# SSD decays from broadcast running sums instead of segment-sum matmuls

## The chip, the cores and the metric

The kernel runs on one core of a Trainium2 chip. The metric is device time in microseconds (us) of one execution. Its engines run side by side, each through its own fixed list of instructions: TensorE (PE, with PEld for its weight loads), VectorE (DVE), ScalarE (ACT), GpSimd (POOL) and SyncE (SP), which here only issues transfers. They wait for each other through semaphores, and each engine works strictly in the order of its list.

## The reference, cut to what matters

Two post-norm layers over 512 tokens and 1024 features: one Mamba-2 (SSD) mixer, one stick-breaking attention, each followed by a squared-ReLU MLP. The change touches the SSD mixer alone. Per head, with `a` the (negative) log decay of each time step, the mixer needs inside a chunk the matrix of decays between every two time steps:

```
def segsum(a):
    cs = jnp.cumsum(a, axis=-1)
    diff = cs[..., :, None] - cs[..., None, :]
    return jnp.where(mask, diff, -jnp.inf)        # mask: lower triangle
...
a = da...                                          # da = softplus(dt) * -exp(a_log)
a_cs = jnp.cumsum(a, axis=-1)
decay_mat = jnp.exp(segsum(a))
cb = jnp.einsum("bclgn,bcsgn->bcgls", cc, bc)
y_diag = jnp.einsum("bcgls,bcgrls,bcsgrp->bclgrp", cb, decay_mat, xc)
decay_states = jnp.exp(a_cs[..., -1:] - a_cs)
...
y_off = jnp.einsum("bclgn,bcgrpn,bcgrl->bclgrp", cc, prev, jnp.exp(a_cs))
```

There are 32 heads in 8 groups of 4; a group shares its B and C. All sums are over float32 values and the kernel keeps float32 accuracy.

## The kernel before, in words

**Numbers and matmuls.** Every float32 operand of a matmul is split in two: a high part rounded to the fast format (`fp32r`) and the rest, the low part. One product is then three matmuls (`mm3`, lines 208 to 210: high by high, low by high, high by low). Weights come in pieces of 128x1024 in the order of the list `stream`: SP fetches a piece into `wr` (tag raw, two buffers), ACT casts it to `wh` (line 191), and DVE, or POOL for one piece in four, subtracts to `wl` (line 193). `wh` and `wl` have four buffers each, so the cast of a piece waits until PE has finished with the piece four places earlier.

**Order of the work.** The program is traced as plain Python and a scheduler then fixes the list of each engine, taking pieces that are traced earlier first where it can; so the order on an engine is not the order of the text. Tile pools (`bufs=n`) set how many copies of a tile can be alive; PSUM has the tags `mm` and `bg` with four buffers each.

**The SSD mixer** (`ssm`) handles the sequence as four chunks of 128 tokens (`c` = 0 to 3) and the heads as eight groups (`g` = 0 to 7). Before the groups, `time_steps` projects the time steps (`pdt`, 24 matmuls), transposes them (`pdtt`), computes softplus on small 128x128 tiles (`dtt1`, a chain of some twenty short DVE and ACT instructions, lines 636 to 648), and makes `da` = dt * a in two parts, `da_h` and `da_l`. From these it forms on PE the running sums over a chunk, `pacs` (a matmul with the triangle `tri_le`), and the totals, `ptot` (with ones); ACT turns them into `E`, `bdec` and `dec_s`.

For each group there are five projections of 24 (or 48 half-width) matmuls: B and C (`in_bc`: `pB`, `pC`), z (`in_z`: `pz`) and two for x (`in_x`: `px`). A projection of B, C or x is followed by a convolution (one ACT instruction at line 678, then three on DVE at line 680, the tile `ca_...`) and a SiLU. `in_xt` transposes x (`pxt`) and makes the scaled copies `dx`, `xd`, `xe`.

`decays` makes the decay block of each chunk, 128 rows s by 4 heads by 128 columns t. For chunk c: POOL selects twice (line 779), from `da_h` and from `da_l`, each spread along t by a zero step, zero where t < s: the tiles `dm`. PE multiplies both with the triangle `tri_gt` (lines 782 and 783), which sums over s < k <= t into the PSUM tile `sg`; ACT takes the exponential into the SBUF tile `dec` (line 785). `scores` makes the products C.B of the group (`cb`, 12 short matmuls), copies them to `cbm` (line 795), and POOL zeroes the upper part (line 796). `front` multiplies `dec` by `cbm` (line 807; DVE for chunks 0 to 2, POOL for chunk 3), splits the product into `W_h` (ACT, line 809) and `W_l` (DVE, line 810), and advances the state (`st`, `pv`, `pr`). `back` uses `W` and `pr` on PE (`py`, `po`) and gathers `yg`; `gate` and `finish` follow.

The loop over g runs `scores`, `front` and `back` of group g while the object `fill` deals out projection steps of group g+1 between them: `fill.run(4)` gives four steps of three matmuls. After the chunks come `in_xt` of the next group, `gate`, `decays` of the next group, and `finish`. After groups 3 and 7 the output projection `tok_out` (`so`) runs half the sum each.

Of the kernel before, what the change touches and what calls it, by code (L numbers as in the profile page):

```python
# [23 lines left out]
G = 8  # L24
# [11 lines left out]
def trunk(ctx: ExitStack, tc: tile.TileContext, io):  # L36
# [6 lines left out]
    ps = ctx.enter_context(tc.tile_pool(name="ps", bufs=4, space=PSUM))  # L43

# [22 lines left out]
    for _ in range(14):  # L67
# [6 lines left out]
    tri_gt = cp.tile([P, P], F32R, name="tri_gt")  # L74
    nc.gpsimd.affine_select(tri_gt, one, pattern=[[-1, P]], compare_op=ALU.is_gt, fill=0.0,
                            base=0, channel_multiplier=1)
# [71 lines left out]
    depth = [2]  # L148

# [57 lines left out]
    def mm3(out, a, b, start, stop, skip=False):  # L207
        nc.tensor.matmul(out, a[0], b[0], start=start, stop=False, skip_group_check=skip)  # L208
        nc.tensor.matmul(out, a[0], b[1], start=False, stop=False, skip_group_check=skip)  # L209
        return nc.tensor.matmul(out, a[1], b[0], start=False, stop=stop, skip_group_check=skip)  # L210
# [362 lines left out]
    def ssm(sp, nxt_ln):  # L573
# [49 lines left out]
        dec_s = small("dec_s")  # L623

        def time_steps():
            w = wdt
            pd = psum("mm", [P, T], "pdt")
            proj(pd, w, x_)
# [25 lines left out]
            nc.vector.tensor_sub(da_l, da, f(da_h))  # L654
            pa = psum("bg", CH, "pacs")
            pt_ = psum("bg", CH, "ptot")
            for o, l in ((pa, tri_le), (pt_, ones_r)):
                nc.tensor.matmul(o, l, da_h, start=True, stop=False)
                nc.tensor.matmul(o, l, da_l, start=False, stop=True)
            nc.scalar.activation(E, pa, AF.Exp)  # L660
# [109 lines left out]
        def decays(q, cs=range(NT)):  # L770
            g = q.g
            hs = slice(4 * g, 4 * g + 4)
            if cs[0] == 0:
                q.dec = []
            for c in cs:
                nm = f"{g}_{c}"
                dm = pair(f"dm{nm}", S4, "dm", 1)
                for o, i in zip(dm, (da_h, da_l)):
                    nc.gpsimd.affine_select(o, f(i[:, c, hs]).unsqueeze(2).to_broadcast(S4), pattern=[[0, 4], [1, P]],
                                            compare_op=ALU.is_ge, fill=0.0, base=0, channel_multiplier=-1)  # L780
                pseg = psum("bg", S4, f"sg{nm}")
                nc.tensor.matmul(pseg, tri_gt, dm[0], start=True, stop=False)
                nc.tensor.matmul(pseg, tri_gt, dm[1], start=False, stop=True)
                dec = sp.tile(S4, F32, tag="dec", name=f"dec{nm}", bufs=4)
                table_order("exp", nc.scalar.activation(dec, pseg, AF.Exp))
                q.dec.append(dec)
# [516 lines left out]
```

## Time and profile before

| | us |
|---|---|
| median of 3 runs | 1417.35 (1416.71 to 1418.65) |
| the profiled execution, its own time | 1416.35 |
| its span, first to last instruction | 1414.2 |
| PE busy in the span | 1389.0 |
| DVE busy | 1076.8 |
| ACT busy | 783.8 |
| POOL busy | 221.8 |

The profile is of one execution. Busy time is the time in which an engine's instructions run; a wait is put down to what ended it. PE's matmuls overlap: one of 512 columns lasts 0.39 us but the next starts 0.23 us after it, and it is the second number that counts in a row of matmuls. The SSD mixer takes about the first 470 us of the span: preparation to about 49 us, groups 0 to 3 to about 217 us with some 45 us each, `tok_out`, groups 4 to 7, `tok_out`. The granted TensorE clock was 0.997 on average.

### The profile page before, as it was taken

How to read it: one execution, taken by the hardware profiler on the slowest of the kernel's cores; microseconds unless marked ns; L12 is line 12 of the kernel's file. 1: busy time of each engine (PE TensorE's matmuls, PEld its weight loads, DVE VectorE, ACT ScalarE, POOL GpSimd, SP SyncE). 2: the span in 40 equal slices, each digit the busy share in tenths (PEclk: the TensorE clock that was granted, in tenths of full speed). 3: DMA queues.
4: the chain of work that ended last, by engine and by line, in shares of the span. 5: the costliest groups of instructions: out<-in, count | busy, mean ns of one | idle time of the engine just before them, and what ended most of it. 6: DMA issues, size and time to landing. Idle time of an engine off the chain costs nothing.

```text
span 1414.2 us, 19327 instructions
## 1 busy us (share of the span) xinstructions
PE 1389.0 (98%) x7414; PEld 1197.0 (85%) x7414; DVE 1076.8 (76%) x1530; ACT 783.8 (55%) x1264; POOL 221.8 (16%) x249
## 2 busy tenths in 40 slices
PE   9999999999999999999999999999999999999996
PEld 6898897889997988888888799899889888888885
DVE  5798898368887596785859868787877966858588
ACT  5556575246653363635445568898853636454463
POOL 2344555034443100000000200000000000000001
PEclk9999999999999999999999999999999999999998
DMA  5223222222223345455453521121223455454533
GB/s 186 76 77 133 70 66 75 89 81 70 74 65 107 115 162 169 159 162 166 134 169 116 163 90 47 44 75 46 75 90 120 134 179 164 149 168 139 168 116 123
DMA packets 46699, 162.99 MB, mean 115 GB/s; under 512 B 5520, under 2 KB 5776, under 8 KB 46608
## 3 DMA queue, kind: packets, MB, share of 16 engines
q1 hardware_dynamic: 44016, 157.44, 34.9%
q10 hardware_dynamic: 2592, 4.33, 1.0%
q8 instruction: 58, 0.95, 0.3%
q14 instruction: 33, 0.27, 0.1%
HBM read 159.65 MB, written 2.10 MB: 114 GB/s over the span
## 4 chain that ended last, share of the span: by engine, by line
PE 87%; DVE 7%; ACT 2%; DMA 2%; issue 1%; POOL 1%; ACTq 0%; SPq 0%; DVEq 0%; POOLq 0%
PE f L209 8%; PE f L210 8%; PE f L208 8%; PE X L210 3%; PE X L208 3%; PE X L209 3%; PE pz L208 2%; PE pz L210 2%; PE pz L209 2%; PE px L208 2%; PE px L209 2%; PE px L210 2%; PE Y L210 2%; PE Y L209 2%; PE Y L208 2%; PE z L1141 1%
## 5 line engine op out<-in xcount | busy, mean ns | idle before, releaser
L191 ACT CAST wh<-wr 128x1024 fp32r<-128x1024 f32 x235 | 246.6, 1050 | 326.1 <-DMA wr<-w 159.1
L193 DVE TENSOR_TENSOR wl<-wr,wh 128x1024 fp32r<-128x1024 f32 x218 | 268.6, 1233 | 181.6 <-ACT wh L191 180.8
L210 PE MATMUL f<-ln_hh,wl 128*128 128x512 f32 (+1 forms) x544 | 201.2, 371 | 0.0
L209 PE MATMUL f<-ln_hl,wh 128*128 128x512 f32 (+1 forms) x544 | 201.2, 371 | 0.0
L208 PE MATMUL f<-ln_hh,wh 128*128 128x512 f32 (+1 forms) x544 | 200.3, 371 | 0.0
L210 PEld LDWEIGHTS f<-ln_hh,wl 128*128 128x128 f32 x544 | 102.4, 188 | 17.8 <-DVE wl L193 0.4
L209 PEld LDWEIGHTS f<-ln_hl,wh 128*128 128x128 f32 x544 | 102.4, 188 | 17.7 <-DVE ln_hl L400 0.2
L208 PEld LDWEIGHTS f<-ln_hh,wh 128*128 128x128 f32 x544 | 102.0, 188 | 17.4
L348 POOL TENSOR_TENSOR ln_rs<-ln_sums 128x1 f32<-128x1 f32 (+1 forms) x6 | 3.1, 513 | 632.6 <-ACT lnr L346 632.6
L208 PE MATMUL X<-wh,hP 128*128 128x512 f32 x192 | 74.7, 389 | 0.0
L209 PE MATMUL X<-wl,hP 128*128 128x512 f32 x192 | 74.7, 389 | 0.0
L210 PE MATMUL X<-wh,l 128*128 128x512 f32 x192 | 74.0, 389 | 0.0
L210 PE MATMUL pz<-wh,x_l 128*128 128x256 f32 x256 | 72.7, 284 | 0.0
L209 PE MATMUL pz<-wl,x_h 128*128 128x256 f32 x256 | 72.6, 284 | 0.0
L208 PE MATMUL pz<-wh,x_h 128*128 128x256 f32 x256 | 72.4, 283 | 0.0
L461 ACT CAST hP<-r 128x512 fp32r<-128x512 f32 x80 | 48.1, 620 | 32.0 <-DVE r L473 31.1
L193 POOL TENSOR_TENSOR wl<-wr,wh 128x1024 fp32r<-128x1024 f32 x17 | 42.6, 2504 | 92.3 <-ACT wh L191 92.0
L208 PE MATMUL px<-x_h,wh 128*128 128x512 f32 x128 | 50.8, 397 | 0.0
L209 PE MATMUL px<-x_l,wh 128*128 128x512 f32 x128 | 50.3, 393 | 0.0
L210 PE MATMUL px<-x_h,wl 128*128 128x512 f32 x128 | 50.2, 392 | 0.0
L209 PE MATMUL Y<-wl,hP 128*128 128x512 f32 x128 | 49.8, 389 | 0.0
L209 PEld LDWEIGHTS pz<-wl,x_h 128*128 128x128 f32 x256 | 48.8, 190 | 0.9
(1365 smaller groups left out, 3923.0 us busy)
## 6 DMA issues: line engine op xcount, KB each, us to landing
wr<-w SPq DMA_DIRECT2D x160, 512.0 KB, 3.6
wr<-w_bc SPq DMA_DIRECT2D x16, 512.0 KB, 3.5
wr<-w_x SPq DMA_DIRECT2D x16, 512.0 KB, 3.5
wr<-w_z SPq DMA_DIRECT2D x16, 512.0 KB, 3.5
wr<-w_so SPq DMA_DIRECT2D x16, 512.0 KB, 3.5
rawa<-w SPq DMA_DIRECT2D x16, 512.0 KB, 3.7
rawc<-w SPq DMA_DIRECT2D x16, 512.0 KB, 4.4
wr<-w_qk SPq DMA_DIRECT2D x16, 512.0 KB, 3.5
```

The costliest lines, as they stand in the source:

```text
L191: nc.scalar.copy(hi, raw)
L193: eng.tensor_sub(lo, raw, f(hi))
L208: nc.tensor.matmul(out, a[0], b[0], start=start, stop=False, skip_group_check=skip)
L209: nc.tensor.matmul(out, a[0], b[1], start=False, stop=False, skip_group_check=skip)
L210: return nc.tensor.matmul(out, a[1], b[0], start=False, stop=stop, skip_group_check=skip)
L348: nc.gpsimd.tensor_add(rs, self.sq[:, t0:t1, 0], self.sq[:, t0:t1, 1])
L461: nc.scalar.copy(h, src)
L1141: w_end[0] = nc.tensor.matmul(zj, ntri_ge, x, start=False, stop=i == 1, skip_group_check=True).ins
```

## The change

The exponent of the decay block is now a difference of running sums, cs[t] - cs[s], as in the reference, with no matmul for it.

- `time_steps` gets two more short matmuls that form the running sums with heads and chunks on the partitions (`pcsr`), ACT copies them (`csr`), and SP writes them, 128x128 numbers, to a scratch in device memory, `cs_rows`. ACT also stores the negative running sums, `ncs` = -`pacs`.
- `spread(q, c)` replaces the making of `dm` and `sg`: SP reads the 512 running sums of chunk c and the four heads from `cs_rows` into all 128 partitions of a `dec` tile, DVE adds `ncs` (its own row's sum, spread along t), and POOL selects once, putting -1e30 where t < s. `decays` is then only the four exponentials on ACT. The 64 matmuls `sg`, the `tri_gt` triangle, and the select of `cbm` are gone; `front`'s product is on DVE for all four chunks.
- `dec` has six buffers and not four. The spreads of group g+1 are traced behind `front(q, c)` of group g, chunk by chunk. Where `tok_out` follows (between groups 3 and 4), the exponentials of the next group are traced behind `finish` and not ahead of it.
- At the start the projections of B and C of group 0 are traced interleaved with that of the time steps. The later half of `time_steps` (the sums and what follows) is traced behind the last matmul of B's projection of group 1, which is drawn ahead (`ahead`, `tc.issue_after(behind[0])`: PE may not issue the sums before that matmul).

```diff
-        def time_steps():
-            w = wdt
-            pd = psum("mm", [P, T], "pdt")
-            proj(pd, w, x_)
+        ncs = small("ncs")
+        cs_rows = dp.tile([NT, H, P], F32, name="cs_rows")
+
+        def time_steps(pd):
...
             nc.vector.tensor_sub(da_l, da, f(da_h))
+            yield
             pa = psum("bg", CH, "pacs")
             pt_ = psum("bg", CH, "ptot")
             for o, l in ((pa, tri_le), (pt_, ones_r)):
                 nc.tensor.matmul(o, l, da_h, start=True, stop=False)
                 nc.tensor.matmul(o, l, da_l, start=False, stop=True)
+            pr = psum("mm", [P, P], "pcsr")
+            for i, x in enumerate((da_h, da_l)):
+                nc.tensor.matmul(pr, x.rearrange("p c h -> p (c h)"), tri_le, start=i == 0, stop=i == 1)
+            rows = sp.tile([P, P], F32, name="csr")
+            nc.scalar.copy(rows, pr)
+            nc.sync.dma_start(cs_rows.rearrange("c h t -> (c h) t"), rows)
+            nc.scalar.activation(ncs, pa, AF.Copy, scale=-1.0)
...
-        def decays(q, cs=range(NT)):
+        def spread(q, c):
             g = q.g
-            hs = slice(4 * g, 4 * g + 4)
-            if cs[0] == 0:
+            if c == 0:
                 q.dec = []
-            for c in cs:
-                nm = f"{g}_{c}"
-                dm = pair(f"dm{nm}", S4, "dm", 1)
-                for o, i in zip(dm, (da_h, da_l)):
-                    nc.gpsimd.affine_select(o, f(i[:, c, hs]).unsqueeze(2).to_broadcast(S4), pattern=[[0, 4], [1, P]],
-                                            compare_op=ALU.is_ge, fill=0.0, base=0, channel_multiplier=-1)
-                pseg = psum("bg", S4, f"sg{nm}")
-                nc.tensor.matmul(pseg, tri_gt, dm[0], start=True, stop=False)
-                nc.tensor.matmul(pseg, tri_gt, dm[1], start=False, stop=True)
-                dec = sp.tile(S4, F32, tag="dec", name=f"dec{nm}", bufs=4)
-                table_order("exp", nc.scalar.activation(dec, pseg, AF.Exp))
-                q.dec.append(dec)
+            dec = sp.tile(S4, F32, tag="dec", name=f"dec{g}_{c}", bufs=6)
+            nc.sync.dma_start(dec.rearrange("p h t -> p (h t)"),
+                              cs_rows[c, 4 * g:4 * g + 4, :].rearrange("h t -> (h t)").partition_broadcast(P))
+            nc.vector.tensor_tensor(dec, dec, ncs[:, c, 4 * g:4 * g + 4].unsqueeze(2).to_broadcast(S4), op=ALU.add)
+            nc.gpsimd.affine_select(dec, dec, pattern=[[0, 4], [1, P]], compare_op=ALU.is_ge, fill=-1e30,
+                                    base=0, channel_multiplier=-1)
+            q.dec.append(dec)
+
+        def decays(q):
+            for dec in q.dec:
+                table_order("exp", nc.scalar.activation(dec, dec, AF.Exp))
...
             nc.scalar.copy(q.cbm, pcb)
-            nc.gpsimd.affine_select(q.cbm, q.cbm, pattern=[[0, NT], [1, P]], compare_op=ALU.is_ge, fill=0.0,
-                                    base=0, channel_multiplier=-1)
...
-            eng = nc.gpsimd if c == 3 else nc.vector
-            eng.tensor_tensor(dec, dec, q.cbm[:, c, :].unsqueeze(1).to_broadcast(S4), op=ALU.mult)
+            nc.vector.tensor_tensor(dec, dec, q.cbm[:, c, :].unsqueeze(1).to_broadcast(S4), op=ALU.mult)
...
         cur = Group(0)
-        time_steps()
-        run(in_bc(cur, 0))
-        run(in_bc(cur, 1))
+        pd = psum("mm", [P, T], "pdt")
+        b_steps, c_steps = in_bc(cur, 0), in_bc(cur, 1)
+        for k, _ in enumerate(proj_steps(pd, wdt, x_)):
+            next(b_steps)
+            if k >= KD // 2:
+                next(c_steps)
+                next(c_steps)
+        steps = time_steps(pd)
+        next(steps)
+        run(b_steps)
+        run(c_steps)
         run(in_x(cur, 0))
         run(in_x(cur, 1))
+        ahead = Group(1)
+        b_steps = in_bc(ahead, 0)
+        for _ in range(KD):
+            next(b_steps)
+        with tc.issue_after(behind[0]):
+            run(steps)
+        for c in range(NT):
+            spread(cur, c)
         decays(cur)
...
+            def first(c):
+                front(q, c)
+                if nxt:
+                    spread(nxt, c)
...
-            if nxt:
+            if nxt and g % 4 < 3:
                 decays(nxt)
             finish(q, 1 if nxt else 2)
+            if nxt and g % 4 == 3:
+                decays(nxt)
```

Three places show what moves. In the lists a number behind a name is the tile's own; a digit in `pB1`, `pC1`, `px01` is the group (and half). The line numbers are those of each kernel's own text.

The first place is PE at the end of the preparation. Before, with most of C's projection of group 1 (`pC1`) ahead of the sums:

```order
L208 MATMUL pC1_553<-x_h_115,wh5_364 128x512
L209 MATMUL pC1_553<-x_l_116,wh5_364 128x512
L658 MATMUL pacs_224<-da_h_164,tri_le_98 128x128
L658 MATMUL ptot_225<-da_h_164,ones_r_76 128x128
L659 MATMUL pacs_224<-da_l_165,tri_le_98 128x128
L659 MATMUL ptot_225<-da_l_165,ones_r_76 128x128
L710 MATMUL pbt0_276<-ident_93,ca_B0_266 128x128 x3
L782 MATMUL sg0_0_403<-dm0_0h_399,tri_gt_100 128x512
L783 MATMUL sg0_0_403<-dm0_0l_400,tri_gt_100 128x512
L210 MATMUL pC1_553<-x_h_115,wl5_365 128x512
L208 MATMUL pz00_618<-wh6_485,x_h_115 128x256
```
After, beginning with the last matmuls of B's projection of group 1 (`pB1`):

```order
L207 MATMUL pB1_396<-x_h_115,wh4_318 128x512
L208 MATMUL pB1_396<-x_l_116,wh4_318 128x512
L209 MATMUL pB1_396<-x_h_115,wl4_319 128x512
L659 MATMUL pacs_421<-da_h_164,tri_le_100 128x128
L659 MATMUL ptot_422<-da_h_164,ones_r_78 128x128
L663 MATMUL pcsr_427<-tri_le_100,da_h_164 128x128
L743 MATMUL pxt00_471<-ident_95,ca_x00_347 128x128
L743 MATMUL pxt00_471<-ident_95,ca_x01_384 128x128
L743 MATMUL pxt00_471<-ident_95,ca_x00_347 128x128
```
The 24 matmuls of `pB1` stand ahead of the sums in both; the 23 of `pC1` that stood between them and the sums now stand behind, and the transposes `pxt` come between the sums of `da_h` and those of `da_l`.

The second place is DVE where it finishes the time steps. Before, from the end of the convolution of the second x tile of group 0 (`ca_x01`):

```order
L680 SCALAR_TENSOR_TENSOR ca_x01_393<-px01_368,cw_72,ca_x01_393 128x509
L646 SCALAR_TENSOR_TENSOR dtt1_201<-dtt1_201 128x128
L648 SCALAR_TENSOR_TENSOR dt_163<-dtt1_201 128x128
L652 SCALAR_TENSOR_TENSOR dtt2_202<-dt_163,dtt2_202 128x128
L653 CAST da_h_164<-dtt2_202 128x128
L654 TENSOR_TENSOR da_l_165<-dtt2_202,da_h_164 128x128
L193 TENSOR_TENSOR wl8_623<-wr8_620,wh8_622 128x1024
L664 TENSOR_TENSOR dtt2_202<-ptot_225,dtt2_202 128x128
L713 TENSOR_TENSOR bt0l_281<-pbt0_276,bt0h_280 128x384
L680 SCALAR_TENSOR_TENSOR ca_B1_529<-pB1_489,cw_72,ca_B1_529 128x511
L680 SCALAR_TENSOR_TENSOR ca_B1_529<-pB1_489,cw_72,ca_B1_529 128x510
L680 SCALAR_TENSOR_TENSOR ca_B1_529<-pB1_489,cw_72,ca_B1_529 128x509
```
After, from the split of a weight piece (`wl8`) on:

```order
L192 TENSOR_TENSOR wl8_599<-wr8_596,wh8_598 128x1024
L645 SCALAR_TENSOR_TENSOR dtt1_265<-dtt1_265 128x128
L688 SCALAR_TENSOR_TENSOR ca_B1_514<-pB1_396,cw_74,ca_B1_514 128x511
L645 SCALAR_TENSOR_TENSOR dtt1_265<-dtt1_265 128x128
L688 SCALAR_TENSOR_TENSOR ca_B1_514<-pB1_396,cw_74,ca_B1_514 128x510
L646 SCALAR_TENSOR_TENSOR dtt1_265<-dtt1_265 128x128
L688 SCALAR_TENSOR_TENSOR ca_B1_514<-pB1_396,cw_74,ca_B1_514 128x509
L648 SCALAR_TENSOR_TENSOR dt_163<-dtt1_265 128x128
L652 SCALAR_TENSOR_TENSOR dtt2_266<-dt_163,dtt2_266 128x128
L653 CAST da_h_164<-dtt2_266 128x128
L654 TENSOR_TENSOR da_l_165<-dtt2_266,da_h_164 128x128
```
The convolution `ca_B1`, which reads the finished projection `pB1` from PSUM, stood behind `da_h` and now stands ahead of it, woven into the chain of `dtt1`.

The third place is DVE around the first decay blocks. Before:

```order
L742 TENSOR_TENSOR xd0_435<-xt00_445,xd0_435 128x8x64
L680 SCALAR_TENSOR_TENSOR ca_C1_608<-pC1_553,cw_72,ca_C1_608 128x510
L742 TENSOR_TENSOR xd0_435<-xt01_458,xd0_435 128x8x64
L807 TENSOR_TENSOR dec0_0_406<-dec0_0_406,cbm0_480 128x512
L807 TENSOR_TENSOR dec0_1_415<-dec0_1_415,cbm0_480 128x512
L807 TENSOR_TENSOR dec0_2_424<-dec0_2_424,cbm0_480 128x512
L745 TENSOR_TENSOR xt00_445<-xt00_445,dec_s_168 128x512
L680 SCALAR_TENSOR_TENSOR ca_C1_608<-pC1_553,cw_72,ca_C1_608 128x509
L193 TENSOR_TENSOR wl11_849<-wr11_846,wh11_848 128x1024
L745 TENSOR_TENSOR xt01_458<-xt01_458,dec_s_168 128x256
L810 TENSOR_TENSOR W0_0l_504<-dec0_0_406,W0_0h_503 128x512
L810 TENSOR_TENSOR W0_1l_559<-dec0_1_415,W0_1h_558 128x512
```
After:

```order
L785 TENSOR_TENSOR dec0_1_445<-dec0_1_445,ncs_169 128x512
L785 TENSOR_TENSOR dec0_2_451<-dec0_2_451,ncs_169 128x512
L785 TENSOR_TENSOR dec0_3_457<-dec0_3_457,ncs_169 128x512
L688 SCALAR_TENSOR_TENSOR ca_C1_584<-pC1_538,cw_74,ca_C1_584 128x511
L756 TENSOR_TENSOR xe0l_469<-xt01_490,xe0h_468 128x256
L785 TENSOR_TENSOR dec1_0_566<-dec1_0_566,ncs_169 128x512
L810 TENSOR_TENSOR dec0_0_439<-dec0_0_439,cbm0_512 128x512
L688 SCALAR_TENSOR_TENSOR ca_C1_584<-pC1_538,cw_74,ca_C1_584 128x510
L785 TENSOR_TENSOR dec1_1_623<-dec1_1_623,ncs_169 128x512
L810 TENSOR_TENSOR dec0_1_445<-dec0_1_445,cbm0_512 128x512
L688 SCALAR_TENSOR_TENSOR ca_C1_584<-pC1_538,cw_74,ca_C1_584 128x509
L813 TENSOR_TENSOR W0_0l_553<-dec0_0_439,W0_0h_552 128x512
```
The five additions of `ncs` (each behind its transfer) stand ahead of the first product with `cbm0`; a sixth stands ahead of the first `W0_0l`.

More of the change, by code (lines that the diff above doesn't have):

```diff
@@ L43, in trunk @@
     ps = ctx.enter_context(tc.tile_pool(name="ps", bufs=4, space=PSUM))
+    dp = ctx.enter_context(tc.tile_pool(name="dp", bufs=1, space=bass.MemoryType.DRAM))
     def psum(tag, shape, name):
@@ L73, in trunk @@
                             base=0, channel_multiplier=-1)
-    tri_gt = cp.tile([P, P], F32R, name="tri_gt")
-    nc.gpsimd.affine_select(tri_gt, one, pattern=[[-1, P]], compare_op=ALU.is_gt, fill=0.0,
-                            base=0, channel_multiplier=1)
     none_r = cp.tile([P, P], F32R, name="none_r")
@@ L148, in trunk @@
     depth = [2]
+    behind = [None]
     def emit_w():
@@ L209, in mm3 @@
         nc.tensor.matmul(out, a[0], b[1], start=False, stop=False, skip_group_check=skip)
-        return nc.tensor.matmul(out, a[1], b[0], start=False, stop=stop, skip_group_check=skip)
+        end = nc.tensor.matmul(out, a[1], b[0], start=False, stop=stop, skip_group_check=skip)
+        behind[0] = end.ins
+        return end
     def proj(out, w, r, c0=0, c1=T):
@@ L895, in ssm @@
                 yT = act_pair(f"yT{g}")
-            nxt = Group(g + 1) if g + 1 < G else None
+            nxt = (Group(g + 1) if g else ahead) if g + 1 < G else None
             q = cur
             if nxt:
-                fill.add(in_bc(nxt, 0))
+                fill.add(in_bc(nxt, 0) if g else b_steps)
                 fill.add(in_bc(nxt, 1))
@@ L904, in ssm @@
                 fill.add(in_x(nxt, 1))
+            def first(c):
+                front(q, c)
+                if nxt:
+                    spread(nxt, c)
             scores(q)
             fill.run(4)
-            front(q, 0)
+            first(0)
             fill.run(5)
-            front(q, 1)
+            first(1)
             fill.run(5)
@@ L912, in ssm @@
             fill.run(4)
-            front(q, 2)
+            first(2)
             fill.run(4)
@@ L916, in ssm @@
             fill.run(4)
-            front(q, 3)
+            first(3)
             fill.run(4)
@@ L946, in ssm @@
                 else:
-                    nxt_ln.load_rows(lambda j, c0: sp.tile(S4, F32, tag="dec", name=f"lnr{j}{c0}", bufs=4)
+                    nxt_ln.load_rows(lambda j, c0: sp.tile(S4, F32, tag="dec", name=f"lnr{j}{c0}", bufs=6)
                                      .rearrange("p a c -> p (a c)"), T)
```

## The prediction

> **What bounds the kernel now.** I read the page first (shares of busy time, then the chain that ended last).
>
> ```profile
> PE 1389.0 (98%) x7414; PEld 1197.0 (85%) x7414; DVE 1076.8 (76%) x1530; ACT 783.8 (55%) x1264; POOL 221.8 (16%) x249
> ...
> PE 87%; DVE 7%; ACT 2%; DMA 2%; issue 1%; POOL 1%; ACTq 0%; SPq 0%; DVEq 0%; POOLq 0%
> ```
>
> PE is busy for 98% of the span and carries 87% of the chain: a matmul that goes is time gained, unless PE then waits. Next came PE's waits in the first 475 us, the SSD mixer (waited for, total, times, longest).
>
> ```profile
> PE pyt L872 <- DVE yg L867: 1.4, 1, 1.4
> ...
> PE st L208 <- ACT dec L785: 1.0, 1, 1.0
> ```
>
> Apart from the first 16 us and the output projections these are the only ones over 0.4 us. So every new wait of PE counts in full. The stretches from one group's score product to the next (length; then busy PE, PEld, DVE, ACT, POOL; groups 1, 2, 3, 5, 6) show which engine is next:
>
> ```profile
> 106.10:150.80 44.70, 42.76 (x267) 37.79 (x265) 40.81 (x63) 27.29 (x50) 22.65 (x24) 1.00 0.34 117
> 150.80:193.40 42.60, 42.60 (x269) 38.14 (x267) 37.23 (x63) 27.09 (x50) 22.11 (x22) 1.00 0.24 75
> 193.40:237.10 43.70, 43.70 (x256) 38.28 (x254) 35.58 (x53) 24.27 (x45) 24.12 (x23) 1.00 0.20 61
> 327.80:372.80 45.00, 45.00 (x290) 40.70 (x288) 37.86 (x61) 27.51 (x49) 22.15 (x23) 1.00 0.23 71
> 372.80:413.10 40.30, 40.30 (x289) 37.73 (x287) 34.14 (x57) 26.08 (x49) 19.68 (x22) 1.00 0.21 66
> sum 216.30, PE 214.36 PEld 192.64 DVE 185.62 ACT 132.24 POOL 110.70; mean PE 42.87 PEld 38.53 DVE 37.12 ACT 26.45 POOL 22.14
> ```
>
> DVE is busy for 185.6 of 216.3 us, 86%, in group 1 for 91%. ACT and POOL are at 61% and 51%. The change takes from PE and gives to DVE.
>
> **PE's gain.** What the removed matmuls cost is their step in the chain, not their length:
>
> ```profile
> 48.49 0.35 PE pbt L710 x3
> 48.84 0.23 PE sg L782
> 49.07 0.23 PE sg L783
> ...
> 49.54 0.12 PE pz L208
> ```
>
> and their number stands in the answer on the tile `sg`, eight rows of eight, of which the first and the last are:
>
> ```profile
> L782 PE MATMUL sg<-dm_0h,tri_gt x8: 393/476/481, 48.6 to 398.9; 128*128 128x512 f32 x8
> ...
> L783 PE MATMUL sg<-dm_3l,tri_gt x8: 389/477/485, 59.9 to 412.6; 128*128 128x512 f32 x8
> ```
>
> 64 x 0.23 = 14.7 us off PE, 1.84 per group, all on the path. The wait of `st` for `dec` (1.0) falls too: it was for a PSUM buffer that `sg` held. Added are two 128-column matmuls `pcsr`, 2 x 0.12 = 0.2 us. Net -15.5 before any new wait.
>
> **First new wait: the sums behind `pB1`.** The lists show that PE now issues `pacs` right behind `pB1`, while DVE has the convolution of that same `pB1` ahead of `da_h`, which `pacs` reads. So PE must stand still from the end of `pB1` until the convolution and the rest of the chain are through. Before, five microseconds of `pC1` lay there. The rows, of PE (first), ACT (three, of which the first is a cast of a weight piece that waited for PE) and DVE:
>
> ```profile
> 42.71 0.39 PE L208 MATMUL pC<-x_h,wh 128*128 128x512 f32 x1
> ```
> ```profile
> 48.17 1.05 ACT L191 CAST wh<-wr 128x1024 fp32r<-128x1024 f32 x1 [2.12 <-PE pC L209]
> 49.24 1.28 ACT L660 ACT_TABLE_LOAD   x1
> 50.53 0.28 ACT L660 ACTIVATE E<-pacs 128x128 f32<-128x128 f32 x1
> ```
> ```profile
> 40.59 1.22 DVE L193 TENSOR_TENSOR wl<-wr,wh 128x1024 fp32r<-128x1024 f32 x1
> 41.72 0.28 DVE L645 SCALAR_TENSOR_TENSOR dtt<-dtt 128x128 f32<-128x128 f32 x1
> 41.92 0.74 DVE L680 SCALAR_TENSOR_TENSOR ca_x<-px,cw,ca_x 128x511 f32<-128x511 f32 x1
> 42.59 0.28 DVE L645 SCALAR_TENSOR_TENSOR dtt<-dtt 128x128 f32<-128x128 f32 x1
> ...
> 44.62 0.29 DVE L648 SCALAR_TENSOR_TENSOR dt<-dtt 128x128 f32<-128x128 f32 x1
> 44.95 0.29 DVE L652 SCALAR_TENSOR_TENSOR dtt<-dt,dtt 128x128 f32<-128x128 f32 x1
> 45.27 0.23 DVE L653 CAST da_h<-dtt 128x128 fp32r<-128x128 f32 x1
> ```
>
> PE's first row is where `pB1` had ended, 42.71. Three transposes `pbt` (0.35) move ahead of that point, so it ends at 43.06 now. ACT, in its order, first casts the piece `wh8`, whose buffer `pB1` holds until its end: 43.1 to 44.1. The convolution's ACT part runs meanwhile behind it. DVE has `wl8` next: 1.13 from one start to the next (45.3), then 0.20 for a step of the small chain, three convolution steps of 0.67 with two small ones between (47.9), `dt` 0.33, `da` 0.32, `da_h` 0.23: 48.8. PE waits 48.8 - 43.1 = 5.7 us. No row of before shows this wait, but its length follows from the order; it could be down to 5.0 if ACT takes the convolution early and `wl8` hides, up to 7 if DVE is late on arrival, which the order makes possible: two more pieces of work (`bt0l` and a third weight piece) lie ahead of it now. I take 5.7.
>
> **Second new wait: the way through device memory.** From 48.8 PE has 3 short sums, 8 transposes, 8 matmuls of `pC1`, 3 sums again; with 0.12 and 0.23 that ends at 52.3. Then 16 of `pC1` (3.7), 12 of `cb` (1.4), 80 half-width ones of `pz` (9.6) and 9 short ones (1.1): PE comes to the first `py`, which needs `W0_0l`, at 68.1. The other way: ACT stores `ncs`, loads a table (1.28), forms `E`, `bdec`, a copy and `csr`, each 0.28 or less: about 2.2 us, to 54.5. Then a write and a read, one after the other. No transfer of before is of this kind; the nearest rows are (KB each, median us to landing; and a queue with packets, MB, share of 16 engines):
>
> ```profile
> lnr<-lnrow ACTq DMA_DIRECT2D x12, 256.0 KB, 3.4
> ...
> out<-v SPq DMA_DIRECT2D x8, 256.0 KB, 2.0
> ```
> ```profile
> q10 hardware_dynamic: 2592, 4.33, 1.0%
> ```
>
> `lnr` is the same shape as a spread, one row into 128 partitions; `out` is a write four times as large. So the write lands at 56.5 and the first spread at 59.9. Each further one takes the engines 1% of 1414 us for 4.33 MB, or 0.85 us for 0.26 MB, so six have landed by 64.2. DVE then has ahead of the end of `W0_0l`: six additions, two products and `W0_0l` itself, 9 instructions of 128x512 with two operands, three steps of a convolution (2.0) and two small pieces (0.7). The nearest row for the nine:
>
> ```profile
> L807 DVE TENSOR_TENSOR dec<-dec,cbm x24: 676/680/2878, 66.8 to 420.6; 128x512 f32<-128x512 f32 x24
> ```
>
> 0.68 at the median, less the 0.07 by which neighbours overlap above, is 0.61 each: 5.5. Together 8.2 and about 0.5 for landings that come later than DVE: 68.6. PE would wait 0.5 us. The maximum of that row, 2.88, shows that such an instruction can take 2.2 more. I take 1.5; the ends are 0 (the write is small) and 5 (each transfer a microsecond slower and one such delay). Behind `W0_0l` come some nine microseconds of DVE until `pr0_0l` (eight at 0.61, two weight pieces at 1.13, six short ones), which PE needs 8.7 us after it starts `py` (by its list: 25 matmuls at 0.23, 16 at 0.12 and a dozen short ones); I put 1.0 there, 0 to 3.
>
> **DVE in the groups.** Each group gets four additions of `ncs` and the fourth product from POOL: 5 x 0.61 = 3.05 us. Over the five stretches DVE then needs 185.6 + 15.3 = 200.9 of 216.3 - 9.2 = 207.1 us, 97%, and in group 1 43.9 of 42.9. POOL's load falls (per group eight selects, the select of `cbm` and a product go, four selects come), which should shorten DVE's long cases. I take 0.5 us per group of new waiting for six groups, 3.0; the ends are 0 and 4.9 per group (DVE keeps all the idle time that it has, so each group grows by 3.05 where it should have fallen by 1.84).
>
> [...]
>
> **What costs nothing.** SP gets 33 more transfers, in the queue of the weights, and waits there for `dec` buffers with weight pieces behind. Cover: SP already waits far longer for the buffers of those pieces,
>
> ```profile
> SPq L167 <- DVE wl L193: 199.2, 34, 12.1
> ```
>
> so 33 x 0.85 = 28 us of transfers in some 400 fit. Without it a late spread holds DVE, about 1 us each. The exponentials stay 32 on ACT. POOL's work is off the path.
>
> **The sum.** -14.7 - 1.0 + 0.2 + 5.7 + 1.5 + 1.0 + 3.0 = -4.3. Against the profiled execution's own 1416.35 that is 1412.0; that execution lies 1.0 below the median of the runs, and I do not add this. About 0.2% (2.8 us) is what a measurement of this kernel tells from no change.
>
> **The rivals.**
> - *DVE becomes the bound* (slower). If DVE in each group keeps the 3.9 us of waiting it has in group 1, the five groups need 47.8, 44.2, 42.5, 44.8 and 41.1 us where PE needs 42.9, 40.8, 41.9, 43.2 and 38.5 (busy time + 3.05 + 3.9, and length - 1.84): 13.2 us, with a sixth group like these 15.8 and not 3.0. That gives 1425. It decides from about 3 us of kept waiting. For it: 97%. Against it: POOL's relief, and that the idle time above was partly slack.
> - *The cover holds better*: only the first wait is real, the rest is absorbed: -15.5 + 5.7 = -9.8, 1406.6. For it: PE had almost no wait at 86%. Against it: DVE's added work.
> - *The way through memory is slow*: the second wait is at its end of 5: 1415.5. For it: two dependent transfers, neither seen here. Against it: the `pz` cover of ten microseconds.
>
> **How the numbers follow.** Forecast 0.43 (1408.5 to 1415.5; four fifths of it faster by over 0.2%, the rest within), better cover 0.18 (nearly all faster), slow memory 0.12 (within), DVE-bound 0.25 (0.04 within, 0.21 slower), something unseen 0.02. So faster 0.52, within 0.2% 0.25, slower 0.23. The range 1406 to 1422 takes in the better cover at its low end and half of the DVE-bound case. The likeliest case gives 1412.
>
> **What would show it.** In the trace after: no `sg`; PE idle 5 to 7 us ahead of `pacs`, put down to `da_h`; a wait of `py` for `W_0l` of 0 to 5 us; DVE busy above 90% in group 1, with its time waiting for transfers of `dec` under 1 us each; stretches between score products some 1.5 us shorter. The prediction is wrong if `pacs` does not wait (then 1406), or if PE waits for DVE's `wl`, `W` or `pr` by microseconds in each group (then 1420 and more).

## The result, and the profile after

The changed kernel is slower. Its median is 1433.87 us (1433.37 to 1434.70, four runs) against 1417.21 us of before, measured beside it (1416.71 to 1418.65, four runs): a ratio of 1.0117, with an interval of 1.0103 to 1.0131. The forecast was 1412.0 with a range of 1406 to 1422. Each experiment below has its ratio to runs of before taken beside it; the medians of those runs lie between 1416.6 and 1417.5 us, so differences of about 1 us between experiments say nothing. A single run, 1961.3 us at a granted clock of 0.65 (the kernel with both edits and the bias, below), stands far from all others and no reading rests on it. The profiled execution after has a span of 1432.2 us, 18.0 more than before; the first matmul of the first MLP starts at 487.2 us where it started at 469.2, so the whole difference of these two executions lies in the SSD mixer.

The page of after, its row of engines and its row of the granted clock:

```profile
PE 1387.5 (97%) x7352; PEld 1195.5 (83%) x7352; DVE 1085.3 (76%) x1570; ACT 782.6 (55%) x1266; POOL 181.4 (13%) x200
...
PEclk9989999999999999999999999999999999999998
```

PE is still busy for 97%, and its busy time fell by only 1.5 us though 64 matmuls of 0.23 us are gone. The clock row says why to look further: its third slice (71 to 107 us) is 8, and no slice before the last was under 9 apart from that. Next PE's waits in the first 480 us (waited for, total, times, longest):

```profile
PE pbt L718 <- ACT ca_B L690: 7.9, 2, 7.6
PE pacs L659 <- DVE da_h L653: 6.3, 1, 6.3
PE pyt L875 <- DVE yg L870: 6.2, 4, 2.3
```

The sums wait for `da_h` as forecast. A second wait of 7.6 us stands not at `py` but at `pbt`, the transposes of B of group 1. And `pyt`, which waited once for 1.4 before, now waits four times. The next answer of after gives the granted clock by stretch (length; busy PE, PEld, DVE, ACT, POOL; clock; DMA share and GB/s):

```profile
31.00:48.30 17.30, 13.09 (x61) 10.49 (x58) 15.55 (x32) 12.94 (x18) 2.40 (x1) 1.00 0.39 112
48.30:55.10 6.80, 4.70 (x17) 4.22 (x18) 4.84 (x11) 0.62 (x1) 0.00 (x0) 0.50 0.17 67
55.10:75.60 20.50, 15.73 (x115) 14.70 (x113) 11.35 (x16) 8.53 (x17) 6.40 (x6) 1.00 0.39 106
75.60:85.80 10.20, 7.41 (x34) 7.41 (x35) 10.19 (x17) 6.14 (x11) 3.31 (x3) 0.50 0.32 105
```

Within each of the two long waits (44.1 to 50.4 us and 70.8 to 78.4) the clock falls to 0.50, and it stays there for 7 and for 10 us in all, so that the matmuls behind the wait run slowly too. It is so again at 256.5 to 263.3 and at 454.5 to 457.9; before, the mixer had no such stretch. What this does to a matmul is seen in the list of PE (start, length, instruction):

```profile
43.48 0.39 PE L208 MATMUL pB<-x_l,wh 128*128 128x512 f32 x1
43.70 0.39 PE L209 MATMUL pB<-x_h,wl 128*128 128x512 f32 x1
...
53.25 0.63 PE L208 MATMUL pC<-x_l,wh 128*128 128x512 f32 x1
53.68 0.63 PE L209 MATMUL pC<-x_h,wl 128*128 128x512 f32 x1
```

From one start to the next it is 0.22 us ahead of the wait and 0.43 behind it. Busy time hides this: a slow matmul counts as busy.

So PE's time up to the first `f` was split in three, for each kernel of the study, from the starts of all its matmuls: each step from one start to the next is compared with the median step of matmuls of that width in the same trace. What the medians add up to is "matmul steps"; what a step takes more while the clock is 0.50, up to once the median, is "half clock"; all the rest is waiting. The medians in the table are of all runs, the other columns of the one profiled execution; for "sums behind six projections" that was the fastest run (1422.0 us), for "fourth product on POOL" the slowest (1418.9).

| kernel | median us | first `f` at | matmul steps | half clock | waits and rest |
|---|---|---|---|---|---|
| before | 1417.2 | 469.2 | 448.1 | 0 | 21.1 |
| after | 1433.9 | 487.2 | 433.7 | 9.4 | 44.1 |
| sums behind six projections | 1423.1 | 473.9 | 433.8 | 5.2 | 34.9 |
| the same, fourth product on POOL | 1416.0 | 470.4 | 433.8 | 3.0 | 33.6 |
| the same, additions on ACT too | 1409.9 | 463.7 | 433.6 | 3.0 | 27.1 |
| before, with DVE's added load alone | 1425.8 | 479.1 | 447.9 | 5.5 | 25.7 |

The removed matmuls are worth 14.4 us in the steps, as forecast; 9.4 us at half clock and 23.0 us of waiting stand against them. PE's list names most of that waiting: the two waits of the start, and `pyt`. The three kernels in the middle and the last are experiments, below.

### The profile page after: what moved, and what is told of

It is laid out like the page before. It is cut to its first block, busy times and chain, and to the rows that moved or that the text cites. A ratio compares the mean times of both kernels' runs of the same rounds, so it can differ in the third digit from the quotient of the medians.

```text
span 1432.2 us, 19279 instructions
## 1 busy us (share of the span) xinstructions
PE 1387.5 (97%) x7352; PEld 1195.5 (83%) x7352; DVE 1085.3 (76%) x1570; ACT 782.6 (55%) x1266; POOL 181.4 (13%) x200
## 5 line engine op out<-in xcount | busy, mean ns | idle before, releaser
L209 PE MATMUL px<-x_h,wl 128*128 128x512 f32 x128 | 50.4, 394 | 0.0
L207 PEld LDWEIGHTS pz<-wh,x_h 128*128 128x128 f32 x256 | 49.6, 194 | 0.3
```

Source lines behind the costliest of these rows:

```text
L209: end = nc.tensor.matmul(out, a[1], b[0], start=False, stop=stop, skip_group_check=skip)
```

## The experiments

Theories. **A**: the loss is made at the start, by the two waits and the half clock behind each. **B**: DVE's added work in the groups turns PE's gain into waiting. **C**: the way through device memory sets the start. **D** (against a part of A): a wait costs its length and the clock behind it nothing more.

### The start: position of the sums, and the way through memory

Three kernels, with after the four corners of a square. First the sums are held behind the projection of C of group 1 as well, which stood ahead of them before:

```diff
-        b_steps = in_bc(ahead, 0)
-        for _ in range(KD):
-            next(b_steps)
+        b_steps, c_steps = in_bc(ahead, 0), in_bc(ahead, 1)
+        for s in (b_steps, c_steps):
+            for _ in range(KD):
+                next(s)
...
-                fill.add(in_bc(nxt, 1))
+                fill.add(in_bc(nxt, 1) if g else c_steps)
```

> The changed kernel with one thing moved: the sums stand behind six projections (C of group 1 too), so that the 6.3 us wait of PE for da_h is covered. Theory A (the waits at the start, and the half clock that follows each, make most of the loss): the wait ahead of pacs falls under 1 us and the half clock of 48 to 55 us goes; the way through device memory still ends at the same time, so PE waits for it some 5 to 8 us. About 8 us faster than the changed kernel, 1426, and still slower than before. Theory B (VectorE's added work in the groups is the bound): the start is absorbed later, 1432 to 1435. Theory C (the round trip through memory alone sets the start, what PE does ahead of it does not matter): the second wait grows by what the first loses, 1433.

Measured: 1423.11 us (1421.97 to 1424.18), ratio to before 1.0046 (1.0029 to 1.0063); 10.8 us off after. Its waits of PE:

```profile
PE pyt L875 <- DVE yg L870: 7.2, 3, 5.0
...
PE pacs L659 <- DVE da_h L653: 0.9, 1, 0.9
PE pbt L718 <- ACT ca_B L690: 0.6, 1, 0.6
```

Both waits at the start are down to under 1 us, and no stretch at half clock is left ahead of 235 us. Theory A asked for 8 us and a second wait of 5 to 8 that did not come; theory C is refuted in this place, for the transfers are all still there.

Second, after's start with the old way for group 0 alone (in `decays`: for `q.g == 0` the selects into `dm`, `sg` and the exponential of before; `cbm` selected for that group):

```diff
...
-        for c in range(NT):
-            spread(cur, c)
         decays(cur)
```

> The changed kernel, with the decays of group 0 alone by the old way (8 sg matmuls, selects of dm and cbm); groups 1 to 7 take the spread rows. The first wait stays. Theory A: the wait of pbt (7.6 us) and the half clock of 76 to 86 us (3.5 us lost beside waiting) go, sg costs 1.8: 9 us faster than the changed kernel, about 1425. Theory B: 1434 to 1437 (sg comes on top). Theory C: about 1428, since the round trip was 7.6 of the loss and the clock nothing.

Measured: 1427.64 us (1425.97 to 1428.35), ratio 1.0074 (1.0059 to 1.0089), 6.2 off after: theory C's number, 3 short of A's. The wait of `pbt` is gone, that of `pacs` (6.4) stands, with a stretch of 10.2 us at clock 0.50 that begins in it. Third, both edits:

> Both edits: the sums behind six projections and group 0 by the old way. Theory A: no wait over 1 us and no half clock in the first 100 us; 1417.2 - 12.9 (56 sg) + 0.2 + 5 (pyt waits) + 1 to 3 (later half clock) = about 1412, 1406 to 1417. Theory B: the groups still wait for VectorE, 1425 or more. Theory C: about 1418 (after less 14 of waits less 2, the rest being lost elsewhere).

Measured: 1423.73 us (1423.46 to 1424.17), ratio 1.0048 (1.0033 to 1.0063). That is 0.6 more than with the sums moved alone. So the way through memory costs some 6 us where the sums stand behind five projections, and nothing that shows behind six. (The edit is not the way through memory alone: it puts eight `sg` matmuls back, 1.8 us, and takes four additions off DVE in group 0.) And theory A is short: with no long wait at the start the kernel is still 7 us slower than before, where 5 faster was asked for. Something behind the start takes about 12 us.

### The clock by itself

The control pins C's matmuls of group 1 behind the sums and puts one matmul on constants ahead of them; the next kernel has 36 of those.

```diff
+            pr4 = psum("mm", [P, T], "pcsr")
+            pr = pr4[:, :P]
+            for _ in range(36):          # 1 in the control
+                nc.tensor.matmul(pr4[:, P:].rearrange("p (a c) -> p a c", a=3), ones_r,
+                                 ones_r.unsqueeze(1).to_broadcast([P, 3, P]), start=True, stop=True)
             pa = psum("bg", CH, "pacs")
...
-            fill.run(4)
+            if g == 0:
+                with tc.issue_after(sums_end[1]):
+                    fill.run(4)
+            else:
+                fill.run(4)
```

> Control for the next kernel: the changed kernel, with the matmuls of C of group 1 held behind the sums, and one matmul of 384 columns on constants put into the bank of pcsr ahead of the sums. The wait of PE for da_h stays at 6 to 6.5 us, the clock is halved from about 48 us on. 1430 to 1440 under every theory; it is what the next kernel is compared with.

> As the control, with 36 of these matmuls (0.17 us each, 6.1 us) in the place of one: PE does useless work in the time in which it would wait for da_h, and nothing else changes. Theory A (a wait also costs half the clock afterwards): no half clock at 48 to 55 us; the matmuls behind the sums run at 0.23, the sums reach ScalarE some 2 to 3 us earlier, and the kernel is 2 to 5 us faster than the control. Theory D (a wait costs its own length, no more): within 1 us of the control, or slower by up to 0.5 us where the useless matmuls run past da_h.

(`sums_end[1]` is the last matmul of the sums.) Measured: 1431.52 us (1428.57 to 1434.07) and 1432.05 us (1431.09 to 1433.27): no difference that shows. The same stretch in both, the control first:

```profile
47.20:54.00 6.80, 3.64 (x16) 3.54 (x17) 5.16 (x12) 0.86 (x2) 0.00 (x0) 0.50 0.28 77
```
```profile
47.20:54.00 6.80, 6.73 (x41) 5.86 (x40) 4.70 (x12) 3.06 (x8) 0.00 (x0) 1.00 0.22 78
```

The half clock there went, as theory A says, and the first `py` came at 68.7 and not 71.5 us (0.9 of that difference was there already at the first `px`). But both kernels reach the second group's `cb` at the same time, 110.5 and 110.7: over the mixer some 3.6 us less of half clock stand against waits that did not shrink by the 6 us that the useless matmuls fill, but by 2 (37.6 to 35.6). So the half clock is real, but here it was not what set the end of group 0; the time saved came back as waiting (in the second kernel that `cb` waits 2.4 us for DVE's `xt`, in the control not at all). Theory D's number came out, though not for its reason. Beyond the dummies the two lists differ a little in group 0.

### VectorE's load

Before, with DVE's added load alone:

```diff
+                nc.vector.tensor_tensor(dec, dec, one[:, 0:4].unsqueeze(2).to_broadcast(S4), op=ALU.mult)
                 q.dec.append(dec)
...
-            eng = nc.gpsimd if c == 3 else nc.vector
+            eng = nc.vector
```

> The kernel before, with VectorE's added load alone: each block of decays is multiplied by one on VectorE (512 columns, two operands, as the addition of ncs), and the fourth product goes from GpSimd to VectorE: five instructions of 0.61 us more per group, 24 us in all; sg and everything else stay. Theory B: PE waits for VectorE, 10 us or more slower than before, 1427 and up. Theory A: PE's time with sg leaves VectorE room; the prediction's term was 0.5 us per group, so 2 to 6 us slower than before.

Measured: 1425.83 us (1424.29 to 1427.25), ratio 1.0052 (1.0035 to 1.0069): 8.3 us slower than the runs beside it, between the two theories. In group 1 DVE is now the engine that hardly rests (columns as above):

```profile
109.28:154.97 45.69, 42.95 (x262) 37.59 (x260) 44.36 (x68) 25.90 (x49) 20.34 (x23) 1.00 0.32 114
```

DVE 44.36 of 45.69 us. This is the nearest test of the forecast's term of 3.0, with PE's own work unchanged; the multiplication by one also lengthens the chain from the exponential to the product, and the scheduler's order is another. In the table the loss stands as 5.5 us of half clock and 4.6 of waiting; the longest wait in the mixer that PE's list names is one of 2.1 for `pyt`. Next, in the kernel with both edits, the additions go to ACT as the bias of four exponentials of 128 columns:

```diff
-            nc.vector.tensor_tensor(dec, dec, ncs[:, c, 4 * g:4 * g + 4].unsqueeze(2).to_broadcast(S4), op=ALU.add)
...
-            for dec in q.dec:
-                table_order("exp", nc.scalar.activation(dec, dec, AF.Exp))
+            for c, dec in enumerate(q.dec):
+                for h in range(4):
+                    table_order("exp", nc.scalar.activation(dec[:, h, :], dec[:, h, :], AF.Exp,
+                                                            bias=ncs[:, c, 4 * q.g + h:4 * q.g + h + 1]))
```

> As the kernel with both edits, and the 28 additions of ncs are taken from VectorE: each exponential is issued as four of 128 columns with ncs as their bias, on ScalarE. VectorE loses 28 x 0.61 = 17 us, ScalarE gains about 28 x 0.6 = 17 us. Theory A: within 3 us of the kernel with both edits. Theory B: 5 to 15 us faster than it.

Measured: 1418.44 us, ratio 1.0011 (1.0001 to 1.0021): 5.3 faster than without, at the low end of theory B. Then the load of DVE was taken back whole (the additions to ACT as above, the fourth product to POOL), first with after's start:

```diff
-            nc.vector.tensor_tensor(dec, dec, q.cbm[:, c, :].unsqueeze(1).to_broadcast(S4), op=ALU.mult)
+            eng = nc.gpsimd if c == 3 else nc.vector
+            eng.tensor_tensor(dec, dec, q.cbm[:, c, :].unsqueeze(1).to_broadcast(S4), op=ALU.mult)
```

> The changed kernel with VectorE's load taken back to that of before: the additions of ncs go to ScalarE as the bias of four exponentials of 128 columns, the fourth product goes back to GpSimd. The start stays (sums behind five projections, both transfers). Theory A: the start's loss of some 11 us stays whole, the groups gain what the load cost before, 8 us: 1424 to 1427. Theory B (VectorE's load turns each gain of PE into waiting): the whole loss but the first wait goes, 1417 to 1422, since group 0 has room again to catch up.

Measured: 1427.58 us (1424.82 to 1429.44), ratio 1.0071 (1.0056 to 1.0086). Just above theory A's range, 6.3 off after; the waits at the start stand:

```profile
PE pacs L659 <- DVE da_h L653: 6.3, 1, 6.3
PE pbt L718 <- ACT ca_B L690: 5.2, 2, 3.8
```

The same with the sums behind six projections, and once more with group 0 by the old way:

> The same with the sums behind six projections: nothing is left of VectorE's added load, nor of the first wait. If the start (11 us) and the load (8 us) are the two causes and add up, 1433.9 - 11 - 8 = about 1415; if the removed matmuls then come through whole, 1417 - 14.5 + 3 = 1406. Above 1418 a third cause is missing (the end of group 3, where so was pulled forward).

> The same, and group 0 by the old way (8 sg, no spreads before the first products). Theory C (the round trip costs even behind six projections): 3 to 6 us faster than the kernel without this. Theories A and B: 0 to 2 us slower, by the 1.8 us of sg.

Measured: 1409.87 us (1409.00 to 1410.97), ratio 0.9947 (0.9930 to 0.9963): faster than before and than after, and between the two numbers named ahead of it (1415 and 1406). Its largest waits in the mixer are all under 2 us, and DVE, at 36.18 of 42.50 us in group 1, has room again:

```profile
PE st L208 <- DVE xe4l L756: 1.9, 1, 1.9
PE pbt L718 <- ACT ca_B L690: 1.9, 2, 1.3
PE py L850 <- DVE pv L825: 1.7, 1, 1.7
```
```profile
111.30:153.80 42.50, 41.50 (x264) 37.09 (x263) 36.18 (x58) 28.77 (x60) 17.75 (x18) 1.00 0.43 140
```

The old way for group 0 gives 1415.0 us, ratio 0.9986 (0.9976 to 0.9995), 5 slower: theory C fell a second time, but A and B (0 to 2 slower) missed as well. Its trace has a wait of `pyt` of 5.4 us at the end of group 3, with 10.2 us at clock 0.50 from 233.3 on; the light kernel has neither.

Which half of the relief counts? With the additions moved but the product left on DVE, and with the product moved but the additions left:

> The sums behind six projections, the additions on ScalarE, the fourth product still on VectorE (8 x 0.61 = 5 us of its load): between the kernel with the sums moved alone (1423.1) and the light one. Theory B: 1 to 3 us slower than the light one. Theory A: no difference.

> The sums behind six projections and the fourth product back on GpSimd, the additions of ncs on VectorE. In its order so is still pulled forward in group 3, as in the kernel with the sums moved alone (1423.1). If the product is the load that counts: 1410 to 1413, as the light kernel. If the order at the end of group 3 decides: 1418 to 1423, with a wait of pyt of 4 to 6 us there and half clock after it. If VectorE's whole load decides: between the two, about 1417.

Measured: 1423.18 us (1419.45 to 1427.76), ratio 1.0043 (1.0031 to 1.0054), for the first: a miss for both theories, it gains nothing over the sums moved alone and is 13 slower than the light kernel. And 1415.98 us (1414.05 to 1418.92), ratio 0.9990 (0.9981 to 1.0000), for the second: 7.1 off the sums moved alone, nearest to the number for DVE's whole load (1417). In it, the products on DVE (first row) and the one on POOL, which takes about twice as long (min, median, max in ns):

```profile
L811 DVE TENSOR_TENSOR dec<-dec,cbm x24: 675/680/1749, 68.8 to 422.3; 128x512 f32<-128x512 f32 x24
...
L811 POOL TENSOR_TENSOR dec<-dec,cbm x8: 1288/1298/2835, 71.6 to 419.9; 128x512 f32<-128x512 f32 x8
```

So behind six projections the product gains 7 us alone and 13 together with the additions; the additions gain 6 with the product moved and nothing without. The two are not independent, and they do not go with DVE's busy time. Up to the first `f` DVE is busy for 374.4 us with the sums moved alone, 372.5 with the product moved (7.1 faster), 355.6 with the additions moved (no faster) and 346.4 in the light kernel. The kernel with the additions moved loses in another place: its waits of `pyt` come to 9.5 us (1.4 in the light kernel) and its half clock to 7.9 (3.0), which is 13.0 of the 13.6 us by which its first `f` comes later. So DVE's load, as a number of busy microseconds, is not shown to be the cause; the order in which its results come at the end of a group is part of it.

### The end of group 3

In the kernels with the sums moved, the light one apart, PE draws matmuls of `so` (the output projection) forward into group 3, and `pyt` is left without cover at its end. In the kernel with both edits and the bias this is one wait, the only one of PE listed from 160 to 260 us:

```profile
PE pyt L897 <- DVE yg L892: 6.9, 1, 6.9
```

The first half of `so` was held behind the last `py` of that group, here and with the sums moved alone, and in the light kernel:

```diff
+                last_py[0] = nc.tensor.matmul(py[:, h, 0, :], ...).ins
...
+                    with tc.issue_after(last_py[0]):
+                        out(half)
```

> The kernel with both edits and the bias, and the first half of the output projection held behind the last py of group 3, so that its matmuls cover the end of that group (gate, root, pyt). Theory A: the wait of pyt (6.9 us) in group 3 and the half clock from 235 to 245 us (2.9 us beside waiting) go; what of so stood earlier in the group leaves waits of up to 4 us there. 4 to 9 us faster than the kernel with the bias, 1409 to 1414, and so faster than before. Theory B (VectorE is the bound in every group): the wait only moves to py and po of group 3; within 2 us of it, 1416 to 1420.

Measured: 1421.55 us (1420.36 to 1423.61), ratio 1.0028 (1.0019 to 1.0038), 3 slower than without (2.4 by the two ratios). The wait of `pyt` is gone, and waits inside the group stand in its place, with a stretch of 13.7 us at clock 0.50 among them:

```profile
PE py L872 <- DVE bt4l L724: 2.3, 1, 2.3
PE py L873 <- DVE W_0l L835: 1.0, 1, 1.0
PE py L872 <- DVE yg L866: 0.8, 1, 0.8
```

The two balance in the mixer: its first `f` comes at 468.4 us, without the edit at 468.9. What this execution loses lies behind the mixer, from the first `f` to the end, 950.0 us against 947.5 (945.0 in before and after); why is open.

> The sums behind six projections, so of the first half held behind the last py of group 3, no relief of VectorE. If the end of group 3 decides: the wait of pyt (5.0) and the half clock after it (3.6) go, 1413 to 1417. If VectorE's load decides: the wait moves into the group, to py and po, 1420 to 1424.

Measured: 1417.90 us (1415.11 to 1420.82), ratio 1.0007 (0.9997 to 1.0017): 5.2 faster than with the sums moved alone, without relief of DVE, and between the two numbers named ahead of it (the first `f` comes at 467.5 us, 6.4 earlier). A wait of `po` for `yg` of 3.2 us has come up inside the group.

> The light kernel with so held back too, where its order already has most of so late. Either theory: within 2 us of the light kernel's 1409.9.

Measured: 1410.98 us (1406.86 to 1413.51), ratio 0.9950 (0.9932 to 0.9968): no difference from the light kernel.

So the order at a group's end counts as well: holding `so` back gained 5 us in one kernel and nothing in two others. It cannot be taken apart from the load by these runs, since the scheduler writes another order for each load: in the kernel with only the product moved `so` stands drawn forward too, and no long wait followed. What is shown is the sum of the three edits, from after to the light kernel: 10.8 (start), 7.1 (product) and 6.1 (additions), 24.0 us in all. How much of the last two is DVE's time and how much the order that came with it stays open.

## Why the prediction was wrong, step by step

- **PE's gain, -14.7**: right; the steps of the matmuls fell by 14.4. The wait of `st` for `dec` went too.
- **First new wait, 5.7**: right in place, cause and size (6.3). DVE did what its list said: `da_h` at 50.12 behind the convolution of `pB1`.
- **Second new wait, 1.5 with ends 0 and 5**: wrong in place and size, 7.6 us, by several of its parts. The transfers were taken too short: the write took 3.4 and not 2.0 us, and the six spreads, issued 0.4 to 0.5 us apart, landed between 3.5 and 7.1 us after their issue, up to 1.9 us apart and not 0.85. One of DVE's additions, at 69 us, took 2.7 us where the median is 0.69: the single delay that the upper end had allowed for. And the list of PE was read only for `py`; `pbt` stands ahead of it, and its SiLU stands on ACT behind the first exponentials:

```profile
68.65 0.63 ACT L792 ACTIVATE dec<-dec 128x512 f32<-128x512 f32 x1 [1.15 <-POOL dec L786]
74.72 0.62 ACT L812 CAST W_0h<-dec 128x512 fp32r<-128x512 f32 x1 [5.44 <-DVE dec L810]
75.25 1.15 ACT L792 ACTIVATE dec<-dec 128x512 f32<-128x512 f32 x2
76.41 1.28 ACT L690 ACT_TABLE_LOAD   x1
77.71 0.63 ACT L690 ACTIVATE ca_B<-ca_B 128x512 f32<-128x512 f32 x1
```

  ACT waits for DVE's products, DVE for the spreads, and `ca_B`, which needs none of them, waits behind. The first wait made this worse: partly at half clock, the eight transposes and eight matmuls that stand between the first and second halves of the sums took until 55.7. With the sums behind six projections 0.6 us of it was left. The first experiment took 10.8 us off, start and clock together, where the sum had 5.7 + 1.5 + 1.0 = 8.2; that part was 2.6 short.
- **`pr0_0l`, 1.0**: PE's list names no wait for it, and only one for a low part of `pr` at all (`pr_2l` in group 3, 0.5 us). Within its range of 0 to 3.
- **DVE in the groups, 3.0**: the step that failed. DVE's added instructions cost 8.3 us in before, and in the changed kernel with the sums behind six projections the two edits that take them away are worth 13.2, the order that came with them included. The rival "DVE becomes the bound" had put 15.8 in the place of 3.0 and was given 0.25. But its sign did not come: PE waits for no `wl`, `W` or `pr` by microseconds in a group (0.5 is the longest in the groups of after). What came is the wait of `pyt` at the ends of groups, 6.2 us against 1.4, with half clock behind one of them; the sum had no term for a group's end. DVE was read rightly as nearly full: in after it is busy for 95% of groups 1 and 3 (first and second row),

```profile
114.72:166.44 51.72, 50.34 (x336) 45.96 (x335) 49.05 (x80) 32.66 (x58) 17.59 (x17) 1.00 0.41 137
206.93:254.69 47.76, 45.14 (x270) 39.48 (x269) 45.36 (x73) 27.71 (x51) 20.13 (x17) 1.00 0.33 100
```

  though these stretches hold more work of PE and DVE than those of before, so neither lengths nor busy times are to be compared. POOL's relief, which the prediction set against it, is in the trace. Up to the first `f`, before (first row) and after:

```profile
0.00:469.20 469.20, 459.33 (x2695) 402.31 (x2696) 365.72 (x573) 253.59 (x438) 191.79 (x201) 1.00 0.28 89
0.00:487.20 487.20, 457.97 (x2632) 400.64 (x2633) 374.34 (x613) 251.72 (x440) 151.20 (x152) 0.97 0.33 103
```

  DVE is busy for 8.6 us more, for 40 more instructions that had been reckoned at 0.61 us each, 24.4 in all. Its product with `cbm`, 1.03 us in the mean before, takes 0.68:

```profile
L810 DVE TENSOR_TENSOR dec<-dec,cbm x32: 675/682/684, 74.0 to 438.6; 128x512 f32<-128x512 f32 x32
```

  In before the 13 of its 24 products on DVE during which POOL ran nothing took 0.68 us each, the 11 during which it ran 0.69 to 2.88; in after POOL ran during two of the 32, and these took 0.68 too. Of after's 32 additions the 17 without POOL took 0.67 to 0.69, the 15 with it up to 2.68. So the relief came and the loss came all the same. Why so few added busy microseconds cost so much is open between the load and the order.
- **What costs nothing**: the spreads wait longer than forecast, DVE 15.4 us for them in all,

```profile
DVE dec L785 <- DMA dec<-cs_rows: 15.4, 11, 3.8
```

  and yet, for group 0, cost PE nothing that could be measured behind six projections (1423.73 to 1423.11 and 1415.0 to 1409.87 us, with group 0's spreads away and there).
- **Not in the sum at all**: the clock, 9.4 us of the table. No row of before showed it, whose mixer has no stretch at 0.50. In after there are four: 6.8 us long from 48.3, begun in the wait of 6.3; 10.2 from 75.6, begun in that of 7.6; and 6.8 from 256.5 and 3.4 from 454.5, behind waits of 1.6 and 1.3. In these 27.3 us lie the 9.4.

In the table of after alone the 18.0 us by which its first `f` came later are -14.4 in matmul steps (forecast -14.7 + 0.2), +23.0 in waits (forecast 5.7 + 1.5 + 1.0 + 3.0 - 1.0 = 10.2) and +9.4 at half clock (no term). Put together in the order of the experiments: the light kernel is 7.1 us under before, not 14.5, so 7.4 us are still lost there to waits and half clock; the additions on DVE add 6.1, the product 7.1, the place of the sums 10.8. That is 16.9 over before, and 16.7 was measured. Against the sum, the start was 2.6 short, the load and the order that came with it 10.2, and 7.4 stood in no term. The second alone would have turned the direction (with 13.2 in the place of 3.0 the same sum comes to 1422), and so would the other two together (10.0).

## What to carry to other kernels

When work moves from the engine that is the bound to one at 86 to 91%, half a microsecond of waiting per group is too little to reckon with: here some 3 us of added DVE instructions per group of some 43 us came, with the order that followed from them, to 13.2 of the 14.5 us that 64 removed matmuls gave. The version that gained had DVE's old load (four narrow exponentials with a bias on ACT, which had room, and one product on POOL). Do not measure such an edit by the second engine's busy time alone: 18.7 us less of it gained nothing in one order. Look at what PE waits for at the ends of groups. A sum that others wait for is placed behind as much independent work of PE as its inputs need time; one more projection ahead of it was worth 10.8 us here. And split PE's busy time by the granted clock before believing it.

## What was not expected of the hardware

- The clock fell behind short waits too. The stretches at 0.50 in the mixer of after were 6.83, 10.24, 6.83 and 3.41 us long, those named above for other kernels 6.8, 10.2 (twice) and 13.7: one to four times the shortest. Two of after's begin in its long waits, but it had one behind a wait of 1.3 us, and another behind 1.6:

```profile
454.50:457.90 3.40, 3.40 (x10) 2.63 (x9) 1.72 (x6) 1.71 (x5) 1.61 (x3) 0.50 0.51 158
```
```profile
PE so L207 <- ACT yT4h L878: 1.3, 1, 1.3
```

  while a wait of 2.3 us at 204 us in after, and one of 2.6 in the kernel with the old group 0, had none. The four stretches of after in the mixer begin on one grid of 3.413 us (75.6, 256.5 and 454.5 lie 8, 61 and 119 steps behind 48.3). A point of that grid, 205.3, parts the wait of 2.3 us in 1.1 and 1.2, while the waits of 1.3 and 1.6 lie whole or nearly so in the step ahead of a fall. For these three waits the place on the grid fits what followed, and the length does not. Short transposes and narrow matmuls stood around the waits that were followed by a fall; whether they bear on the fall was not tried.
- Six broadcasts of 256 KB issued 0.4 to 0.5 us apart landed later one after the other, 3.5, 5.1, 6.2, 6.6, 6.9 and 7.1 us after their issue; the median of all 32 was 3.7:

```profile
dec<-cs_rows SPq DMA_DIRECT2D x32, 256.0 KB, 3.7
...
cs_rows<-csr SPq DMA_DIRECT2D x1, 64.0 KB, 3.4
```

  A write of 64 KB to device memory took 3.4 us until its reader could start, longer than the 2.0 of the 256 KB writes of `out`.
- Filling a wait of PE with useless matmuls kept the clock at 1.00 from 47.2 to 54.0 us and gained nothing: the `cb` of the second group then waited 2.4 us for DVE (`xt`), where it had not waited.
